# A hybrid decoder layer on one core: gates by one Silu activation, rotations read out of SBUF, and a planner that issues each instruction when its inputs are there

## The chip, the core and the metric

The kernel runs on one core of one Trainium2 chip. The number that counts is the device time of one execution in microseconds (us), from three runs of the kernel before: 2657.21, 2661.30 and 2662.37, so the median is 2661.3 us. A core has a matrix engine (PE, with its weight loads shown as PEld), a vector engine (DVE), a scalar engine for activations (ACT), a general engine (POOL) and a queue engine that only starts DMAs (SP). Each of them works off its own list of instructions in the order in which they stand in it. If the first one in the list has to wait, all behind it wait too.

## What is computed

The reference is one step of a layer with 1024 prompt tokens and 8 decode tokens, 1032 columns in all, with 2048 features. Cut to what matters:

```python
u = rmsnorm(h, g_ln); z = u @ w_in                      # 2048 x 8320
# group A (16 heads of 64): token shift, decay, delta-rule state, per-head norm
xs = feats + mu_shift * (prev - feats)                  # feats = first 3200 columns of z
y_a, wkv_T = rwkv7_scan(wkv0, r, w, k, v, -kk, kk * a)
y_a = (head_norm(y_a) + bonus) * silu(z[..., OFF_GA:OFF_GA + D_A])
# group B (4 heads of 256): rotated q and k, chunked retention, per-head norm
qb = rotary_every_two(q, pos); kb = rotary_every_two(k, pos) / 16
y_b = head_norm(retention(ret0, qb, kb, vb)) * silu(gb)
h = h + concat(y_a, y_b) @ w_out
h = h + sigmoid(h @ w_ple_gate) * (p @ w_ple)
y = rmsnorm(h, g_final)                                 # and the new states
```

## The kernel before, in words

Activations lie transposed, 128 features on the partitions and the 1032 tokens along the free axis, cut into three groups of 344. A projection block makes 128 output features: for each group, 16 steps of three matmuls (`whi` with the high half of u, `whi` with its low half, `wlo` with the high half), 48 matmuls of 344 columns into one PSUM bank. There are 65 such blocks of `w_in`, then 16 of `w_out` (blocks o0 to o15) and 16 of `w_gate` (g0 to g15). Two blocks of p @ w_ple stand in between, one ahead of o0 and one ahead of g0; they have short groups of six matmuls and use four banks.

The eight PSUM banks are two for projections (`pj`), three for everything short (`g`), two for the chain of group A and the states of group B (`ch`), and one for outputs (`y`). Since `pj` has two banks, a group can start only when the bank of the group before the last has been read out; the reading is called the eviction. What an eviction does depends on the block:

- r, k and v of group A (`shifted`, L840): ACT copies the bank to an SBUF tile `z`, POOL forms a difference, DVE makes the shift.
- the gates (`gate_evict`, L867, eight blocks, and `gb_evict`, L346, eight blocks): ACT writes sigmoid(x) into `sgt` (or `g` for the last block), then DVE multiplies it by x, which it reads from the same bank once more.
- q and k of group B (`rope_evict`, L1308): two halves of a head are two blocks; DVE reads the bank twice and multiplies it with the cosine and sine table `tb`, which a DMA on SP fetches per group; POOL adds the products of the second half to `Q` or `K`.
- o0 to o15 (`h_evict`, L1909): DVE adds the residual, ACT and DVE split the sum into two fp16 halves.

While PE runs projections, background generators feed it short work between two steps: `front_gen` (L970) makes a head pair's inputs, `chain_gen` (L1150) walks the sequential state through 16 chunks, `norm` (L1224) is its head norm, `ret_gen` (L1507) and `post_gen` (L1579) are retention and its norm, `dec_gen` and `dec_a_gen` do the decode tokens. The weights are prepared three steps ahead: `ahead` (L395) loads a block and takes its sum of squares (`wjunk`), a tiny matmul adds it over the partitions (`g<-wsr`), `split_w` (L490) makes `whi` on ACT and `wlo` on DVE.

The order of the instructions is made by a planner in the kernel itself (`Driver`, L64). It walks through the program with its own table of costs and a clock `dv.t`, which follows PE. A background generator yields what it waits for: `when(t, more)` (L656) means "go on when the planner believes tile t is written, and `more` us after that"; `yield "g"` means "when a `g` bank is free". What it issues then is put at the end of the engines' lists. `later(t, fn)` (L521) puts off the second half of an eviction to 1.4 us after `t`, or to the next eviction if that comes first (`flush`, L517). So the numbers in `when` set no time on the chip. They set the place of an instruction in its list.

Around the step from o0 to o1: `chase` (L554) runs o0 through the 16 parts of its input as they get ready, on both `pj` banks and the `y` bank; `first_out` (L1936) then waits until the last part is made (`out_open`, L1888) and evicts. The parts are called `mix`; the last two are made by `gated` (L1619): DVE multiplies by the gate, ACT writes the high half, DVE the low half, six times. o1 waits for the `pj` banks, and for its own weights, whose preparation starts only after that of o0.

All instructions of DVE, ACT and POOL carry the line of one recording helper, L256; matmuls carry L303 and transposes L308; DMAs L226. So the rows below are told apart by tiles.

## Time and profile before

| | us |
|---|---|
| median of three runs | 2661.3 |
| the profiled execution, its own time | 2656.86 |
| its span, first to last instruction | 2655.1 |
| PE busy | 2560.7 |
| DVE busy | 1622.2 |
| ACT busy | 1200.8 |
| POOL busy | 541.4 |

The span of the profiled execution is 1.8 us less than its time. PE is busy for 96% of the span, so the table is read from what PE does not do: the 94 us in which it is idle, and the stretches in which its clock is granted at half. A row of the waits names who ended an idle time of an engine; a row of the timeline has the idle time ahead of an instruction in brackets.

### The profile page before, as it was taken

The page shows a single profiled execution, that of the slowest core. Times are in us where ns is not written, and L with a number is a line of the kernel's source. Part 1 is how long each engine was busy: PE and PEld are TensorE (multiplying, and loading weights), DVE is VectorE, ACT ScalarE, POOL GpSimd, SP SyncE. Part 2 cuts the span into 40 slices and gives each one's busy share as a digit, 9 for nine tenths or more (in the row PEclk, how much of TensorE's full clock was granted, in tenths as well). Part 3 has the DMA queues.
Part 4 walks back from the last instruction along what each step waited for, and adds up shares of the span by engine and source line. Part 5 has one row for each costly group of instructions (what it writes and reads, how often), then busy time and mean ns, then how long its engine had stood idle before and what let it go on. Part 6 is the DMA issues. An engine that isn't in the chain of part 4 may idle for free. (4 is left out here: it accounts for less than half of the span.)

```text
span 2655.1 us, 47348 instructions
## 1 busy us (share of the span) xinstructions
PE 2560.7 (96%) x19480; PEld 1761.7 (66%) x19480; DVE 1622.2 (61%) x3458; ACT 1200.8 (45%) x1901; POOL 541.4 (20%) x558
## 2 busy tenths in 40 slices
PE   7899999999999999999999999999989999999996
PEld 4566666666676666666677676776756666666664
DVE  7559685868777766767446957454554443454434
ACT  7564545454645445462343344534443333353433
POOL 3322231322313132220111301111000000033323
PEclk9999999999999999999999999999999999999998
DMA  7222121221212222223334347443443322432314
GB/s 277 78 66 78 59 75 57 78 73 63 77 64 77 80 77 79 64 67 97 98 113 156 101 158 249 141 139 135 156 151 114 110 98 72 154 126 96 110 66 144
DMA packets 146745, 283.67 MB, mean 107 GB/s; under 512 B 62568, under 2 KB 100520, under 8 KB 131424
## 3 DMA queue, kind: packets, MB, share of 16 engines
q1 hardware_dynamic: 132160, 178.91, 20.6%
q10 hardware_dynamic: 14368, 101.73, 11.3%
q8 instruction: 153, 2.51, 0.4%
q14 instruction: 64, 0.52, 0.1%
HBM read 212.78 MB, written 67.55 MB: 106 GB/s over the span
## 5 line engine op out<-in xcount | busy, mean ns | idle before, releaser
L303 PE MATMUL pj<-u,whi 128*128 128x344 f16 x6176 | 1369.1, 310 | 27.0 <-POOL u L256 10.0
L303 PEld LDWEIGHTS <-whi 128*128 128x128 f16 x9408 | 895.8, 99 | 480.7 <-issue 60.0
L303 PE MATMUL pj<-u,wlo 128*128 128x344 f16 x3088 | 951.0, 310 | 0.3 <-DVE wlo L256 0.2
L303 PEld LDWEIGHTS <-wlo 128*128 128x128 f16 x4704 | 460.9, 98 | 232.0 <-DVE wlo L256 4.7
L303 PE MATMUL pj<-mix,whi 128*128 128x344 f16 x1504 | 331.9, 311 | 6.4 <-ACT whi L256 6.4
L303 PE MATMUL pj<-hh,whi 128*128 128x344 f16 (+3 forms) x1536 | 335.0, 309 | 0.2 <-ACT whi L256 0.2
L256 DVE SCALAR_TENSOR_TENSOR wlo<-raw,so,whi 128x512 f16<-128x512 f32 (+1 forms) x398 | 308.2, 806 | 25.6 <-ACT whi L256 24.8
L256 ACT ACTIVATE wjunk<-raw 128x1024 f16<-128x1024 f32 (+1 forms) x188 | 196.1, 1043 | 158.2 <-DVE raw L256 144.6
L256 ACT ACTIVATE whi<-raw,so 128x1024 f16<-128x1024 f32 (+2 forms) x200 | 218.5, 1121 | 87.9 <-DVE so L256 80.3
L303 PE MATMUL pj<-hh,wlo 128*128 128x344 f16 (+3 forms) x768 | 237.3, 309 | 0.4 <-DVE wlo L256 0.4
L303 PE MATMUL pj<-mix,wlo 128*128 128x344 f16 x752 | 231.0, 311 | 2.4 <-DVE wlo L256 2.4
L256 ACT ACT_TABLE_LOAD x150 | 192.4, 1283 | 3.6 <-PEq L2174 0.7
L256 POOL TENSOR_TENSOR H<-H,sgt 128x344 f32<-128x344 f32 (+3 forms) x45 | 55.1, 1226 | 559.2 <-DVE sgt L256 480.4
L256 DVE TENSOR_TENSOR tm<-LT,Z 128x8 f32<-128x8 f32 (+15 forms) x128 | 135.3, 1057 | 1.1
L256 DVE TENSOR_TENSOR sgt<-sgt,xr 128x344 f32<-128x344 f32 (+3 forms) x48 | 26.2, 545 | 155.9 <-ACT sgt L256 142.1
L256 POOL TENSOR_TENSOR d<-z 128x344 f32<-128x344 f32 (+1 forms) x75 | 70.5, 940 | 245.9 <-ACT z L256 191.7
L256 DVE SCALAR_TENSOR_TENSOR hr<-pj,winv,xr 128x344 f32<-128x344 f32 x47 | 27.0, 575 | 133.2 <-PE pj L303 133.2
L256 ACT ACTIVATE AV<-ch 64x128 f32<-64x128 f32 x120 | 32.2, 268 | 164.4 <-PE ch L303 164.2
L256 DVE SCALAR_TENSOR_TENSOR Sbd<-Sbd,DC,ch 64x64 f32<-64x64 f32 x240 | 66.8, 278 | 60.9 <-PE ch L303 57.6
L256 ACT ACTIVATE z<-pj,winv 128x344 f32<-128x344 f32 x74 | 40.1, 546 | 125.5 <-PE pj L303 105.8
L256 ACT ACTIVATE sgt<-pj,winv 128x344 f32<-128x344 f32 (+4 forms) x93 | 50.5, 542 | 89.2 <-PE pj L303 71.6
L256 POOL TENSOR_TENSOR rl<-y,rh 128x344 fp32r<-128x344 f32 x24 | 27.1, 1128 | 305.3 <-DVE rh L256 252.3
(319 smaller groups left out, 3383.7 us busy)
## 6 DMA issues: line engine op xcount, KB each, us to landing
raw<-in_w_in ACTq DMA_DIRECT2D x63, 1024.0 KB, 5.1
raw<-in_w_out ACTq DMA_DIRECT2D x16, 1024.0 KB, 5.0
raw<-in_w_gate ACTq DMA_DIRECT2D x16, 1024.0 KB, 4.7
x<-in_xT SPq DMA_DIRECT2D x16, 516.0 KB, 10.2
tb<-in_rq SPq DMA_DIRECT2D x24, 344.0 KB, 4.4
tb<-in_rk SPq DMA_DIRECT2D x24, 344.0 KB, 3.6
xr<-in_xT SPq DMA_DIRECT2D x16, 516.0 KB, 4.6
d_h<-hr SPq DMA_DIRECT2D x16, 516.0 KB, 2.9
```

The source lines that it names most:

```text
L256: return f(*a, **k)
L303: PE.matmul(out, lhsT, rhs, **kw)
```

## The change

Silu takes the place of sigmoid and a multiplication: ACT writes x * sigmoid(x) from the bank, and DVE does not touch the bank. A rotation's bank is copied by ACT to a tile `z`, and DVE multiplies out of SBUF. `later` takes a margin, 0.2 us where 1.4 stood. In `front_gen`, `rest_gen`, `norm`, `post_gen` and others a `when` stands ahead of each instruction on another engine, and the margins of most matmuls that wait for a split in two halves go from 1.2 or 1.4 us to 0.2; those for `kq`, `Vt` and `yr` go up to 1.2, 1.2 and 3.5. In `post_gen` the low half is made by DVE, where POOL made it. In the chain the copy `AV` is issued one step later (`put`). A rotation's third table is loaded after the first group's rotation. o1 gets banks of its own (`second_out`: both `ch` banks and a `g` bank), is computed before o0 is evicted, and its weights are loaded and squared ahead, as are those of g1.

```diff
@@ preps
                 if raw is None:
                     raw = load_raw(src)
+                    if late is not None:
+                        dv.spawn(ahead(specs, n + 1))
                     yield
@@ later
-    def later(t, fn):
+    def later(t, fn, more=0.2):
...
-            yield when(t, 1.4)
+            yield when(t, more)
@@ gate_evict
-            S_.activation(sg[:, 0:n], ps[:, 0:n], AF.Sigmoid, scale=inv)
+            S_.activation(sg[:, 0:n], ps[:, 0:n], AF.Silu, scale=inv)
+            if gi == 2:
+                S_.activation(gdec[:, p, :], ps[:, n:gw], AF.Identity, scale=inv)
             def fin():
-                if gi == 2:
-                    V.tensor_scalar(out=gdec[:, p, :], in0=ps[:, n:gw], scalar1=inv, scalar2=None, op0=ALU.mult)
-                V.scalar_tensor_tensor(out=sg[:, 0:n], in0=ps[:, 0:n], scalar=inv, in1=sg[:, 0:n],
-                                       op0=ALU.mult, op1=ALU.mult)
                 SP.dma_start(out=d_gate[p][:, g0:g0 + n], in_=sg[:, 0:n])
@@ norm (of group A)
-        halves(y2, Yh, Yl)
-        yield when(Yl, 1.4)
+        yield when(y2, 0.0)
+        V.tensor_copy(out=Yh, in_=y2)
+        yield when(Yh, 0.0)
+        G.tensor_tensor(out=Yl, in0=y2, in1=Yh, op=ALU.subtract)
+        yield when(Yl, 0.2)
         yield "g"
         yv = gtile()
@@ rope_evict
-            for i in {0: (0, 1), 1: (2,), 2: ()}[gi]:
-                st[i] = fpool("tb").tile([P, 2, GW], F32, name="tb", bufs=2)
...
+            if gi == 0:
+                table_of(0)
+                table_of(1)
...
+            z = zg.tile([P, GW], F32, name="z")
+            S_.activation(z, ps, AF.Identity, scale=inv)
+
+            def fin():
+                rotate()
+                if gi == 0:
+                    table_of(2)
...
-                V.scalar_tensor_tensor(out=dst[:, 0, gs], in0=ps, scalar=inv, in1=tb[:, 0, :], op0=ALU.mult, op1=ALU.mult)
+                    V.tensor_tensor(out=dst[:, 0, gs], in0=z, in1=tb[:, 0, :], op=ALU.mult)
...
+            later(z, fin)
@@ gb_evict
-            S_.activation(g, ps, AF.Sigmoid, scale=inv)
+            S_.activation(g, ps, AF.Silu, scale=inv)
             def fin():
-                V.scalar_tensor_tensor(out=g, in0=ps, scalar=inv, in1=g, op0=ALU.mult, op1=ALU.mult)
@@ cap_gen, ret_gen, dec_a_gen
-        yield when(kq, 0.1)
+        yield when(kq, 1.2)
-                    yield when(Vt, 0.1)
+                    yield when(Vt, 1.2)
-        yield when(yr, 0.4)
+        yield when(yr, 3.5)
@@ post_gen, twice
-            halves(y2[:, 0, 0:gw], hi, lo)
-            yield when(lo, 1.2)
+            halves(y2[:, 0, 0:gw], hi, lo, V)
+            yield when(lo, 0.2)
@@ first_out, second_out
-        while not out_open():
+        def results():
+            while not out_open():
+                yield 0.2
+            evict_all(h_evict(0), *got)
+            done.add("out0")
+        dv.spawn(results())
+        dv.spawn(no_hurry(MAIN["n"] + 4))
+
+    def second_out():
+        hi, lo, inv = W.pop(("o", 1))
+        ps = [chp.tile([P, 512], F32, name="ch"), chp.tile([P, 512], F32, name="ch"), gtile()]
+        for gi, (g0, gw) in enumerate(GROUPS):
+            yield from mm3(ps[gi][:, 0:gw], hi, lo, MX[0], MX[1], KT, g0, gw)
+        while "out0" not in done:
             dv.t += 0.3
             yield
-        evict_all(h_evict(0), *got)
-        dv.spawn(no_hurry(MAIN["n"] + 4))
+        evict_all(h_evict(1), ps, inv)
```

Three places show how the lists change. The first is the list of SP at the end of group A, where the last head pair is inverted (`d_X`, `XN`, `d_Z`, `X`) while the first head's q is rotated. `tb<-in_rq` are its tables. Before:

```order
L226 DMA d_mxa<-Y 128x512
L226 DMA d_X<-tm 64x512
L226 DMA XN<-d_X 32x64x16
L226 DMA d_Z<-Z 128x512
L226 DMA tb<-in_rq 128x2x344 x3
L226 DMA X<-d_Z 32x8x32 x4
```

And of the change, at the same place:

```order
L226 DMA d_gb<-sgt 128x344 x2
L226 DMA tb<-in_rq 128x2x344 x5
L226 DMA d_X<-tm 64x512
L226 DMA XN<-d_X 32x64x16
L226 DMA d_Z<-Z 128x512
L226 DMA tb<-in_rq 128x2x344
L226 DMA X<-d_Z 32x8x32 x8
```

Five of the six tables of this head now stand ahead of the round trip through `d_X`. Before, three stood behind it.

The second place is PE's list at the end of o0 (`mix_20584` and `mix_20608` are its last input part) and the start of o1. Before:

```order
L303 MATMUL y<-mix_20584,wlo 128x344
L303 LDWEIGHTS exact
L303 MATMUL g<-wsr,exact 128x2
L303 LDWEIGHTS whi
L303 MATMUL pj<-mix_20261,whi 128x344
```

Of the change:

```order
L303 MATMUL y<-mix_20608,wlo 128x344
L303 LDWEIGHTS whi
L303 MATMUL ch<-mix_20285,whi 128x344
L303 LDWEIGHTS whi
L303 MATMUL ch<-mix_20285,whi 128x344
L303 LDWEIGHTS wlo
L303 MATMUL ch<-mix_20285,wlo 128x344
L303 LDWEIGHTS exact
L303 MATMUL g<-wsr,exact 128x2
```

o1 goes to `ch`, and the sum of its weights is no longer the last thing ahead of it; the `g<-wsr` here is that of o2.

The third place is ACT's list over the same time: `mix<-Y` are the high halves of the last input parts, `wjunk` and `whi` belong to weights, `y<-Y`, `rs` and `tl` to the last norm. Before:

```order
L256 ACTIVATE rs<-rs 128x344
L256 ACT_TABLE_LOAD
L256 ACTIVATE tl<-eps_rms 128x1
L256 ACTIVATE mix_20566<-Y,sret 128x344
L226 DMA raw<-in_w_out 128x2048
L256 ACTIVATE mix_20566<-Y,sret 128x344 x2
L256 ACTIVATE mix_20584<-Y,sret 128x344 x3
L256 ACTIVATE wjunk,wss_20934<-raw 128x1024 x2
```

Of the change:

```order
L256 ACTIVATE tl<-eps_rms 128x1
L226 DMA raw<-in_w_out 128x2048
L256 ACTIVATE whi<-raw,so_20837 128x1024 x2
L256 ACTIVATE mix_20591<-Y,sret 128x344 x3
L256 ACTIVATE mix_20608<-Y,sret 128x344
L256 ACTIVATE wjunk,wss_20960<-raw 128x1024 x2
L256 ACTIVATE wsr<-wss_20960 128x2
L256 ACTIVATE mix_20608<-Y,sret 128x344
```

The high half of o1's weights stands ahead of all six `mix` activations now, and the squares of o2's weights stand between the fourth and the fifth.

## Rows read from the trace of the kernel before

**Rows 1.** The page: busy time of each engine, share of the span and instructions.

```profile
PE 2560.7 (96%) x19480; PEld 1761.7 (66%) x19480; DVE 1622.2 (61%) x3458; ACT 1200.8 (45%) x1901; POOL 541.4 (20%) x558
```

**Rows 2.** Busy time by stretch: group A, the end of group A, group B, the step to `w_out`, `w_out`. Columns: the stretch, its length, busy us (instructions) of PE, PEld, DVE, ACT and POOL, the granted share of PE's full clock, DMA share, GB/s.

```profile
95.00:1250.00 1155.00, 1140.36 (x9571) 784.84 (x9569) 845.43 (x1819) 577.35 (x926) 280.98 (x329) 1.00 0.23 72
1250.00:1350.00 100.00, 96.19 (x869) 66.68 (x868) 45.65 (x132) 29.79 (x54) 14.47 (x15) 0.97 0.33 99
1350.00:1905.00 555.00, 544.87 (x3817) 394.57 (x3816) 328.19 (x779) 238.05 (x386) 82.80 (x76) 0.99 0.45 151
1905.00:1967.00 62.00, 47.68 (x301) 30.19 (x300) 36.60 (x82) 34.61 (x57) 4.58 (x3) 0.92 0.58 199
1967.00:2250.00 283.00, 283.00 (x1953) 189.92 (x1951) 122.27 (x253) 95.74 (x137) 0.00 (x0) 1.00 0.30 100
```

**Rows 3.** The waits of PE between 95 and 1905 us: PE and its line, who ended the wait, us in total, times, the longest.

```profile
PE pj L303 <- DVE sgt L256: 5.8, 5, 1.9
PE pj L303 <- DVE z L256: 5.2, 2, 3.7
PE pj L303 <- ACT z L256: 2.4, 1, 2.4
PE g L308 <- DMA yr<-d_yd: 2.4, 1, 2.4
PE g L308 <- ACT V L256: 2.1, 2, 1.1
PE g L303 <- POOL rl L256: 1.6, 2, 1.0
...
PE g L303 <- DVE kq L256: 1.4, 2, 0.9
```

**Rows 4.** Timeline at the first rotation's second half (start, length, engine, line, operation, tiles, count, and in brackets the idle time ahead of it and who ended it), and below it the busy time and clock of the stretch behind it, columns as in Rows 2.

```profile
1257.07 5.69 SPq L226 DMA_DIRECT2D tb<-in_rq  x3
...
1261.14 1.06 DVE L256 SCALAR_TENSOR_TENSOR z<-pj,winv,tb 128x344 f32<-128x344 f32 x2 [10.76 <-DMA tb<-in_rq]
...
1262.25 0.47 PE L303 MATMUL pj<-u,whi 128*128 128x344 f16 x2 [3.74 <-DVE z L256]
...
1262.60:1269.40 6.80, 6.80 (x51) 4.22 (x50) 3.80 (x8) 4.45 (x6) 2.71 (x4) 0.50 0.50 123
```

**Rows 5.** Timeline of PE at the decode tokens' `yr`, and the stretch behind it, columns as in Rows 4.

```profile
1546.05 0.99 PE L308 MATMUL g<-con,yr 8*128 8x8 f32 x8 [2.35 <-DMA yr<-d_yd]
...
1545.90:1552.70 6.80, 6.65 (x30) 4.53 (x31) 1.01 (x5) 2.26 (x4) 0.00 (x0) 0.50 1.02 416
```

**Rows 6.** Timeline at the step from o0 to o1: PE, then ACT, then DVE, and the busy time and clock of the stretch.

```profile
1950.57 0.17 PE L303 MATMUL g<-wsr,exact 128*128 128x2 bf16 x1
1957.14 0.75 PE L303 MATMUL pj<-mix,whi 128*128 128x344 f16 x2 [6.40 <-ACT whi L256]
1960.29 0.47 PE L303 MATMUL pj<-mix,wlo 128*128 128x344 f16 x1 [2.40 <-DVE wlo L256]
...
1955.95 2.17 ACT L256 ACTIVATE whi<-raw,so 128x1024 f16<-128x1024 f32 x2
...
1957.29 2.28 DVE L256 TENSOR_TENSOR raw<-raw,rf_mix 128x2048 f32<-128x2048 f32 x1
...
1955.50:1965.70 10.20, 6.16 (x21) 2.98 (x22) 6.21 (x7) 5.22 (x8) 0.00 (x0) 0.50 0.38 125
```

**Rows 7.** Groups of instructions over the whole span: line, engine, operation, output <- inputs, partitions x elements, count | busy us, mean ns of one | idle time before them.

```profile
L256 ACT ACT_TABLE_LOAD x150 | 192.4, 1283 | 3.6 <-PEq L2174 0.7 <-DVE winv L256 0.2
...
L256 ACT ACTIVATE z<-pj,winv 128x344 f32<-128x344 f32 x74 | 40.1, 546 | 125.5 <-PE pj L303 105.8 <-PE g L303 6.5 <-DVE winv L256 5.1
...
L256 POOL TENSOR_TENSOR Yl<-y,Yh 128x512 fp32r<-128x512 f32 x16 | 34.1, 2134 | 217.8 <-DVE Yh L256 217.8
...
L256 POOL TENSOR_TENSOR rl<-y,rh 128x344 fp32r<-128x344 f32 x24 | 27.1, 1128 | 305.3 <-DVE rh L256 252.3 <-DVE h L256 25.1 <-ACT whi L256 18.2
...
L256 DVE SCALAR_TENSOR_TENSOR z<-pj,winv,tb 128x344 f32<-128x344 f32 x48 | 25.3, 567 | 23.8 <-DMA tb<-in_rq 10.8 <-issue 5.5 <-PE pj L303 4.0
...
L256 DVE TENSOR_TENSOR sgt<-sgt,xr 128x344 f32<-128x344 f32 x42 | 21.7, 518 | 133.5 <-ACT sgt L256 119.7 <-issue 13.8
...
L256 DVE SCALAR_TENSOR_TENSOR sgt<-pj,winv,sgt 128x344 f32<-128x344 f32 x37 | 21.0, 568 | 1.4 <-ACT sgt L256 0.9
```

**Rows 8.** Timeline of POOL's subtraction `rl` and of the DVE instruction beside it, at two places.

```profile
1661.25 1.05 DVE L256 SCALAR_TENSOR_TENSOR z<-pj,winv,tb 128x344 f32<-128x344 f32 x2
...
1661.47 0.92 POOL L256 TENSOR_TENSOR rl<-y,rh 128x344 fp32r<-128x344 f32 x1 [3.27 <-DVE rh L256]
...
1906.83 2.15 DVE L256 TENSOR_TENSOR raw<-raw,rf_mix 128x1920 f32<-128x1920 f32 x1
...
1907.09 2.67 POOL L256 TENSOR_TENSOR rl<-y,rh 128x344 fp32r<-128x344 f32 x1 [9.32 <-DVE rh L256]
```

**Rows 9.** Timeline of PE in the short groups ahead of o0 and at the last of o0's 16 steps (nine matmuls), and of DVE at the last `mix`.

```profile
1915.69 0.45 PE L303 MATMUL pj<-pt,whi 128*128 128x344 f16 x2 [2.80 <-DVE g L256]
...
1920.19 0.45 PE L303 MATMUL pj<-pt,whi 128*128 128x344 f16 x2 [0.84 <-DVE sgt L256]
...
1949.26 0.46 PE L303 MATMUL pj<-mix,whi 128*128 128x344 f16 x2
...
1945.89 0.57 DVE L256 SCALAR_TENSOR_TENSOR mix<-Y,sret,mix 128x344 f16<-128x344 f32 x1
```

More of the change, by code (lines that the diff above doesn't have):

```diff
@@ L981, in front_gen @@
             S_.activation(sq, k[:, ts], AF.Square, scale=vcol("k_k", p))
-            halves(sq, rh, rl)
+            yield when(sq, 0.0)
+            V.tensor_copy(out=rh, in_=sq)
             sg, a, Gt = scr(0), scr(1), scr(2)
+            yield "g"
             pw = gtile()
             lora_mm(pw, p, 0, ts)
+            yield when(rh, 0.0)
+            G.tensor_tensor(out=rl, in0=sq, in1=rh, op=ALU.subtract)
+            yield when(pw, 0.0)
             S_.activation(sg, pw, AF.Sigmoid, scale=lsi[:, 0:1], bias=vcol("w0", p))
+            yield when(sg, 0.0)
             V.tensor_tensor_scan(out=Gt, data0=rmask, data1=sg, initial=0.0, op0=ALU.mult, op1=ALU.add, est=1.14)
@@ L1102, in bkn_gen @@
                 tr(ps[:, ci * P:ci * P + P], bk[:, ci, :])
+            yield when(ps, 0.1)
             S_.activation(bn, c4(ps), AF.Copy)
@@ L1117, in rest_gen @@
             rs.append((scr(2 * hf, F32R), scr(2 * hf + 1, F32R)))
-            halves(r[:, hf * HB:hf * HB + HB], *rs[hf])
+            V.tensor_copy(out=rs[hf][0], in_=r[:, hf * HB:hf * HB + HB])
+            yield when(rs[hf][0], 0.0)
+            G.tensor_tensor(out=rs[hf][1], in0=r[:, hf * HB:hf * HB + HB], in1=rs[hf][0], op=ALU.subtract)
             yield
@@ L1161, in a2v, with put @@
                    start=True, stop=True, skip_group_check=True)
+            return ps, None
+        def put(c, ps):
             av = None
@@ L1189, in chain_gen @@
             yield
+            if c < 15:
+                nxt = put(c + 1, nxt[0])
             mm(ps[:, 2 * P:3 * P], bn[:, ci, :], uv[:, ci, :], start=True, stop=True)
@@ L1232, in norm @@
         Y = og.tile([P, HB], F32, name="Y")
+        yield when(yc, 0.0)
         S_.activation(y2, yc, AF.Square)
@@ L1314, in pre @@
                 B[which, h] = (fpool("F3") if q else fp).tile([P, 2, T], F32, name=which, tag="F1" if which == "K" else "F3" if q else "F0")
[L1315 to L1318 removed]
+            if gi == 0:
+                table_of(0)
+                table_of(1)
@@ L1593, in norm @@
             mm_exact(pm[:, 0:gw], ones_r, hi, lo)
+            yield when(pm, 0.0)
             for vh in range(2):
@@ L1605, in norm @@
             mm_exact(pq[:, 0:gw], ones_r, hi, lo)
+            yield when(pq, 0.0)
             rs = one.tile([P, GW], F32, name="rs")
@@ L1609, in norm @@
             if h == 3 and g0:
-                table(AF.Sigmoid)
+                table(AF.Silu)
+            yield when(rs, 0.0)
             V.tensor_tensor(out=Y[:, :, gsl], in0=Y[:, :, gsl], in1=rs[:, 0:gw].unsqueeze(1).to_broadcast([P, 2, gw]), op=ALU.mult)
@@ L1947, in items_out @@
         for m in range(KT):
-            spec.append((("o", m), A["w_out"][m], rf_mix, None, None if m else mix_known, None if m else (lambda: ("gate", 7) in done, None)))
-            run = (lambda m=m: proj_gen(("o", m), MX, h_evict(m))) if m else first_out
+            spec.append((("o", m), A["w_out"][m], rf_mix, None, {0: mix_known, 1: lambda: ("gate", 7) in done}.get(m), None if m else (lambda: ("gate", 7) in done, None)))
+            run = {0: first_out, 1: second_out}.get(m, lambda m=m: proj_gen(("o", m), MX, h_evict(m)))
             it.append((("o", m), run, None, None))
```

73 lines of the change are left out of this document (43 added, 30 removed).

## The prediction, made before the changed kernel ran

> **What bounds the kernel.** I read the page's busy times first: PE is at work for 2560.7 of 2655.1 us [rows 1], so no other engine bounds the whole, and the change takes no matmul away. Only three things can give time back: PE's idle time (94 us), stretches at half clock, and new waits with the other sign. I then asked for busy time by stretch [rows 2]. In `w_out` PE is busy for all 283.00 us with 1953 matmuls, 0.145 us each; nothing is to be had there, and a group of 48 lasts 7.0 us. Idle are 14.6 us in group A, 3.8 at its end, 10.1 in group B and 14.3 in the 62 us around the step to `w_out`. The other 51 us (94.4 less these 42.9) lie at the kernel's two ends and around g0, and the change hardly touches those.
>
> The waits of PE [rows 3] say what the idle time in the middle is: banks of `pj` that DVE or ACT had not read out (5.8, 5.2 and 2.4 us), and short matmuls put too early in PE's list (`yr` 2.4, `V` 2.1, `rl` 1.6, `kq` 1.4). The clock adds to it: after the wait of 3.74 us [rows 4] and that of 2.35 us [rows 5] it is granted at half (1.2 of 2.4 GHz) for 6.80 us each, with PE busy throughout. That costs 3.4 us a time.
>
> **The change, part by part.** All terms are us of PE's time.
>
> *Gates.* 48 DVE multiplications out of PSUM (0.568 each [rows 7]) go, 27 us of DVE, and with them the second reading of the bank. The waits under `sgt` are 5.8 in five times [rows 3]. ACT stays in the way, with 0.55 instead of 0.55 + 0.57 before the bank is free. I take 5.0. For the wait of 2.80 ahead of o0, which DVE's `g` ends [rows 9], only that 0.57 comes off, since both banks wait for ACT first: 0.5. Silu needs a table of its own: the built program has 162 table loads on ACT where 150 stood, 12 at 1.283 [rows 7], 15.4 us of ACT. ACT is at 45% [rows 1], and a bank may stay unread for nearly 7.0 us, so I cost them at nothing. If that cover is missing at every one of them it is 15.4. Bounds: 0 to 6.4, less 15.4.
>
> *Rotations.* ACT gains 48 copies at 0.546 [rows 7], 26.2 us; DVE's 96 instructions stay, 0.567 out of PSUM, 0.518 by the nearest row with both inputs in SBUF [rows 7]. What counts is that the bank no longer waits for the table. At 1257 SP stood behind the round trip through `d_X` and issued three tables late, DVE waited 10.76 for them, and PE 3.74 for DVE [rows 4]. In the new list five tables stand ahead of that trip, and ACT frees the bank without any. The two waits under `z` are 5.2 [rows 3]; with the half clock behind the first 8.6. I take 8.5. Bounds 0 (ACT is as late as DVE was) to 8.6.
>
> *Margins made wider.* `yr` moves by 3.1 against a wait of 2.35: 2.35 and its half clock, 5.75 [rows 5]. `kq` moves by 1.1 against 1.4 in two waits, `Vt` by 1.1 against 2.1 in two [rows 3]. Whole: 9.2; I take 9.0. What stands behind these matmuls in PE's list is projection work, which simply comes first now. Bounds 6 to 9.2.
>
> *Margins made narrower.* In `norm` (16 halves) and `post_gen` (24 sums) the matmul behind a split moves 1.0 to 1.2 closer to it. Everything behind it on PE waits with it if it is early. The 16 subtractions `Yl` on POOL take 2.134 in the mean [rows 7], yet before no wait of PE is put down to them [rows 3]. The 24 `rl` go from POOL (1.128) to DVE, 0.518 by the nearest row [rows 7], so half of that lost margin comes back at once. The bounds are 0 and 16 x 1.2 + 24 x 1.0 = 43. I take 5, since no `Yl` and only two `rl` of 24 were late before. The 1.6 of `rl` I leave as it is. The many new `when`s ahead of ACT, DVE and POOL instructions keep an engine from standing before an input that isn't there; of the 2.4 under ACT `z` I take 1.0 for that.
>
> *The step from o0 to o1.* o0's last matmul is done by 1950.74, and the first 21 of o1 fill the time to 1965.7, when the clock is back at full [rows 6]. They are worth 21 x 0.145 = 3.0, so 11.9 is lost: 6.40 and 2.40 of waits, the rest at half clock. The new list starts o1 on `ch`, its weights ready. What was behind the wait moves ahead of it, though: the product `raw` (2.28), the squares `wjunk` and two `whi` (2.17) [rows 6], which now stand between the last norm and the six `mix` activations. The last `mix` ended at 1946.46 and PE reads it at 1949.26 [rows 9], 2.8 of slack. Bounds: all the new work falls into gaps (0), or all delays the chain (2.28 + 2.17 of ACT and DVE work ahead of it, and as much again for o2's weights between two `mix`: 8.9, less 2.8: 6.1). I take 3 there. DVE's `raw` also stands before the short groups' evictions, where PE already waited 0.84 for DVE [rows 9]: between 0 and 2.3 more, and with the last norm pushed back by ACT's squares I take 3 for all of it. So 11.9 - 6 = 6, with ends at 3.5 and 11.9. g1's earlier weights: 0 to 1, I take 1.
>
> Sum: 5.5 + 8.5 + 9.0 + 1.0 + 6 + 1 - 5 = 26 us. The profiled execution's own time is 2656.86 (span and 1.8 around it); 26 off is 2630.9. The median of the runs is 4.4 higher, the lowest run 0.4. I add 2 and forecast 2633.
>
> **A rule that speaks against the rotations.** At 1906.83 DVE multiplies two SBUF tiles for 2.15, and POOL's `rl` beside it takes 2.67; at 1661.25 DVE's rotation has one input in PSUM, and the same `rl` takes 0.92 [rows 8]. The Trainium skill has a rule for this (SBUF — State Buffer, "Who interferes with whom"): a DVE instruction with two SBUF inputs shares its second read path with POOL, and one of them is blocked for the whole instruction; with one SBUF input it does not. The trace agrees, 2.67 against 0.92. The change gives all 96 rotations two SBUF inputs, in group B, where POOL adds the products.
>
> **Rivals.**
>
> 1. *POOL held up by the rotations.* Each group's pair of DVE products (2 x 0.518) can hold POOL by 1.04. Somebody waits only at a block's end, where retention reads `Q` or `K`: 8 second halves x 1.04 = 8.3, if all of it lands on PE. The time is then 2633 + 8.3 = 2641. For it: the two `rl` rows. Against it: POOL is busy 82.8 of 555 us there [rows 2], and v's blocks lie between a rotation and retention.
>
> 2. *The banks now wait for ACT.* Gates and rotations end under another name, because ACT stands before something else or loads a table. Then 5.5 + 8.5 are lost: 2647. For it: ACT `z` already has a wait of 2.4 [rows 3], and ACT gets 42 us more to do. Against it: that was one wait in 74 such evictions [rows 3, 7].
>
> 3. *Slower: PE waits at the 40 narrow places.* PE works its list in order, so a planner that believes a split ready too early stops the projections each time. If each place paid 0.9 on average, that is 36 in place of my 5: 2633 + 31 = 2664. It decides the sign from 0.78 a place on (31 gained without that term, over 40). For it: `Yl` takes up to double what quiet POOL work takes [rows 7, 8], and a margin of 0.2 does not cover that. Against it: the planner's distances are long where it must also find a free bank, and the 24 are faster on DVE.
>
> 4. *Better:* nothing new waits at o0 or at the narrow places, 26 + 5 + 6 = 37: 2622.
>
> **How the numbers follow.** The forecast 0.52, its own range 2624 to 2642; rival 1 0.10; rival 2 0.16; rival 3 0.10; rival 4 0.12. A measurement of this kernel can tell about 0.2% from no change, 5.3 us; so faster is below 2656, slower above 2666.6. Faster 0.86, within 0.2% 0.07 (half of rival 3 and a little of rival 2), slower 0.07. The range of 8 in 10 leaves out the far end of rival 3 and the best of rival 4: 2614 to 2654.
>
> **What would show it.** Right: no wait of PE under DVE `sgt` or DVE `z` in group A's end, none for `yr`, full clock around 1260 and 1550, and o1's first matmul within a microsecond of o0's last; ACT with 162 table loads and some 41 us more busy time, DVE some 15 less. The wait at the last `mix`, if my 3 is right, stands under DVE `mix` at the end of o0. Wrong: PE waits under `Yl`, `rl` or ACT `z` in many places (rivals 2, 3), a fall of the clock where there was none, or POOL's `Q` and `K` near 1.5 us each with PE waiting for them.

## The result, and the profile after

The changed kernel takes 2675.6 us (median of 4 runs, 2674.9 to 2676.3); the kernel before, beside it, 2660.0 (4 runs). The ratio is 1.0059, 95% interval 1.0041 to 1.0076: slower by 15.5 us where 27 less was forecast. Of five kernels below (a_nofront, p_before, b_put, b_norm and b_shift) one execution each took over 5000 us, and the medians leave it out. The page, answering [rows 1]:

```profile
PE 2576.1 (96%) x19480; PEld 1760.0 (66%) x19480; DVE 1618.9 (61%) x3426; ACT 1242.4 (46%) x1969; POOL 487.7 (18%) x534
```

PE's busy time is up by 15.4 with the same 19480 matmuls, so the loss isn't read from idle time alone. By stretch, answering [rows 2]:

```profile
95.00:1250.00 1155.00, 1135.70 (x9459) 772.15 (x9457) 814.65 (x1749) 594.13 (x946) 247.60 (x329) 1.00 0.23 72
1250.00:1350.00 100.00, 99.67 (x898) 68.40 (x896) 56.66 (x135) 32.30 (x60) 14.78 (x13) 1.00 0.31 94
1350.00:1905.00 555.00, 539.45 (x3784) 387.78 (x3783) 333.19 (x789) 255.34 (x416) 73.03 (x57) 0.99 0.43 145
1905.00:1967.00 62.00, 54.24 (x343) 36.70 (x341) 41.40 (x91) 32.98 (x56) 0.00 (x0) 0.92 0.63 226
```

Group A has 112 matmuls fewer in the same 1155 us, group B 33 fewer in 555; the end of group A has 0.3 us of idle time left. The waits of PE between 95 and 1905 us, answering [rows 3]:

```profile
PE g L303 <- DVE rh L256: 11.9, 5, 3.9
PE ch L303 <- DVE UV L256: 6.2, 12, 1.9
PE ch L303 <- DVE R L256: 5.3, 11, 0.8
PE g L303 <- DMA X<-d_Z: 2.3, 1, 2.3
PE g L308 <- DVE BK L256: 2.1, 7, 1.0
PE pj L303 <- ACT z L256: 1.7, 2, 1.1
PE g L303 <- DMA XN<-d_X: 1.5, 1, 1.5
PE g L303 <- DVE kq L256: 1.1, 1, 1.1
```

`sgt`, DVE `z` and `yr` are gone. In their place PE waits for the retention norms' split (`rh`), for the chain (`UV`, `R`) and for the inversion of group A (`BK`, `X`, `XN`).

The waits that the forecast priced are gone where they were looked for; whether the parts that it credited took them away is taken up further down. At the end of group A [rows 4] ACT reads the bank in 0.55 as soon as PE has filled it, five tables stand ahead of the round trip, and the clock is full, as it is where `yr` was [rows 5]; ACT's list, SP's list, and two stretches:

```profile
1261.16 0.55 ACT L256 ACTIVATE z<-pj,winv 128x344 f32<-128x344 f32 x1 [6.51 <-PE pj L303]
...
1242.61 20.72 SPq L226 DMA_DIRECT2D tb<-in_rq  x5
...
1262.00:1270.00 8.00, 8.00 (x58) 5.36 (x57) 7.20 (x13) 3.58 (x5) 0.00 (x0) 1.00 0.59 194
1545.00:1553.00 8.00, 8.00 (x61) 5.44 (x59) 3.47 (x12) 5.57 (x8) 0.00 (x0) 1.00 0.90 330
```

At the step to `w_out`, o1's first matmul starts 0.14 after o0's last, where 6.40 and 2.40 were lost [rows 6]:

```profile
1973.85 0.31 PE L303 MATMUL y<-mix,wlo 128*128 128x344 f16 x1
1973.99 0.31 PE L303 MATMUL ch<-mix,whi 128*128 128x344 f16 x1
```

What is new, by the timeline. The longest `rh` wait: PE, then DVE, whose list holds the split behind work that waited 4.55 for a DMA, and the stretch behind it:

```profile
1460.29 0.66 PE L303 MATMUL g<-rh,exact 128*128 128x344 f32 x1 [3.88 <-DVE rh L256]
...
1453.40 1.23 DVE L256 TENSOR_TENSOR dtm<-Sa,rows 128x1024 f32<-128x1024 f32 x1 [4.55 <-DMA Sa<-in_swkv]
...
1459.90 0.34 DVE L256 CAST rh<-y 128x344 fp32r<-128x344 f32 x1
...
1460.20:1463.60 3.40, 3.31 (x10) 1.78 (x11) 3.33 (x7) 0.00 (x0) 0.42 (x1) 0.50 0.01 2
```

The split itself takes 0.34 and 0.52; it is late because DVE's list is: between the end of that wait and the split DVE has no pause of more than 0.4. The short groups ahead of o0 and those ahead of g0: DVE, PE, and at g1 the sum of its weights:

```profile
1935.39 2.50 DVE L256 TENSOR_TENSOR raw<-raw,rf_mix 128x128 f32<-128x128 f32 x2
...
1939.21 0.73 PE L303 MATMUL pj<-pt,whi 128*128 128x344 f16 x2 [3.60 <-DVE sgt L256]
...
2294.47 2.49 DVE L256 TENSOR_TENSOR raw<-raw,rf_h 128x128 f32<-128x128 f32 x2
...
2297.50 0.73 PE L303 MATMUL pj<-pt,whi 128*128 128x344 f16 x2 [2.75 <-DVE sgt L256]
...
2366.95 0.16 PE L303 MATMUL g<-wsr,exact 128*128 128x2 bf16 x1 [2.33 <-ACT wsr L256]
```

In both places the row of 2.50 or 2.49 joins the last 128x128 of this block's weights and all 128x2048 of the next block's, taken early. It stands ahead of the evictions of the short groups, and PE waits for the bank.

The groups that answer to [rows 7]:

```profile
L256 ACT ACT_TABLE_LOAD x162 | 207.8, 1283 | 6.0 <-DVE wlo L256 1.8 <-PEq L2233 0.7 <-DVE winv L256 0.4
...
L256 POOL TENSOR_TENSOR K<-K,z 128x344 f32<-128x344 f32 x24 | 29.5, 1246 | 88.3 <-DVE z L256 88.3
L256 POOL TENSOR_TENSOR Q<-Q,z 128x344 f32<-128x344 f32 x24 | 28.4, 1203 | 183.2 <-DVE z L256 183.2
L256 DVE TENSOR_TENSOR z<-z,tb 128x344 f32<-128x344 f32 x48 | 24.7, 514 | 14.1 <-issue 8.0 <-ACT z L256 3.6 <-POOL mf L256 1.6
L256 POOL TENSOR_TENSOR Yl<-y,Yh 128x512 fp32r<-128x512 f32 x16 | 23.9, 1494 | 124.5 <-DVE Yh L256 90.6 <-DVE h L256 33.9
L256 DVE TENSOR_TENSOR rl<-y,rh 128x344 fp32r<-128x344 f32 x24 | 12.4, 518 | 0.8
```

### The profile page after: what moved, and what is told of

Its sections match the earlier page's. It is cut to its first block, busy times and chain, and to the rows that moved or that the text cites. A ratio compares the mean times of both kernels' runs of the same rounds, so it can differ in the third digit from the quotient of the medians.

```text
span 2673.0 us, 47282 instructions
## 1 busy us (share of the span) xinstructions
PE 2576.1 (96%) x19480; PEld 1760.0 (66%) x19480; DVE 1618.9 (61%) x3426; ACT 1242.4 (46%) x1969; POOL 487.7 (18%) x534
## 4 chain that ended last, share of the span: by engine, by line
PE 82%; DVE 11%; DMA 2%; ACT 2%; issue 2%; POOL 1%; SPq 0%; DVEq 0%; ACTq 0%; POOLq 0%
PE pj L303 66%; PE ch L303 7%; PE g L303 6%; PE y L303 2%; PE g L308 1%; DVE wlo L256 1%; DVE H L256 1%; DVE tm L256 1%; DVE AR L256 1%; DVE F L256 1%; DVE Y L256 0%; DMA mf<-d_mxa 0%; DVE dtm L256 0%; DVE Sbd L256 0%; DVE so L256 0%
## 5 line engine op out<-in xcount | busy, mean ns | idle before, releaser
L256 DVE SCALAR_TENSOR_TENSOR wlo<-raw,so,whi 128x512 f16<-128x512 f32 (+1 forms) x398 | 323.9, 846 | 20.8 <-ACT whi L256 20.3
L303 PE MATMUL pj<-mix,whi 128*128 128x344 f16 x1408 | 309.5, 310 | 0.0
L303 PE MATMUL pj<-mix,wlo 128*128 128x344 f16 x704 | 215.3, 310 | 0.0
L256 ACT ACTIVATE z<-pj,winv 128x344 f32<-128x344 f32 x122 | 66.0, 543 | 225.7 <-PE pj L303 218.9
L256 DVE TENSOR_TENSOR tm<-LT,Z 128x8 f32<-128x8 f32 (+15 forms) x128 | 142.5, 1113 | 1.6
L256 POOL TENSOR_TENSOR d<-z 128x344 f32<-128x344 f32 (+1 forms) x75 | 61.8, 824 | 384.1 <-ACT z L256 266.7
L256 DVE TENSOR_REDUCE Z<-tm 128x4 f32<-128x8 f32 (+15 forms) x128 | 86.5, 676 | 4.4
## 6 DMA issues: line engine op xcount, KB each, us to landing
x<-in_xT SPq DMA_DIRECT2D x16, 516.0 KB, 10.2
```

What stands on the lines that cost most here:

```text
L256: return f(*a, **k)
L303: PE.matmul(out, lhsT, rhs, **kw)
```

## Where the time goes, stretch by stretch

PE's 14,256 projection matmuls come in the same sequence in every kernel here, so the start of a given one is a mark. I took numbers 720, 2448, 6048, 6768, 9504, 9792, 11808 and 14112, which start at 155, 500, 1244, 1404, 1912, 1973, 2268 and 2616 us in the trace before, and subtracted that trace from each of the others. Between 1973 and 2268 (`w_out`) every difference is 0.0, so that column is left out. Background work crosses a mark now and then, and a stretch at half clock more or less is 1.7 to 5.1 us; a figure is good to some 3 us. "Order only" is explained with its runs. Medians are in us.

| kernel | median | 155–500 | 500–1244 | 1244–1404 | 1404–1912 | 1912–1973 | 2268–2616 |
|---|---|---|---|---|---|---|---|
| changed | 2675.6 | +15.3 | +1.3 | −9.7 | +9.6 | −5.5 | +6.9 |
| p_after (order only) | 2654.7 | +8.6 | +1.4 | −10.1 | +1.8 | −6.6 | +3.9 |
| p_after2 (order only) | 2658.2 | +13.5 | +1.3 | −8.2 | −4.7 | −3.9 | +2.5 |
| a_post12 | 2660.8 | +14.2 | +1.4 | −10.1 | −1.6 | −6.9 | +6.0 |
| a_put | 2671.2 | +8.4 | +3.1 | −9.4 | +12.5 | −6.6 | +4.3 |
| a_nofront | 2677.2 | +13.3 | −0.9 | −3.8 | +13.1 | −5.5 | +6.8 |
| a_nonorm | 2653.1 | +11.4 | −4.7 | −9.3 | +1.4 | −6.6 | +6.0 |
| a_noshift | 2663.6 | +15.0 | +3.5 | −8.4 | +3.3 | −6.7 | +6.0 |
| a_later14 | 2660.0 | +17.2 | +1.2 | −6.5 | −6.7 | −6.6 | +5.9 |
| before | 2657 to 2660 | 0 | 0 | 0 | 0 | 0 | 0 |
| p_before (order only) | 2649.1 | +0.3 | −0.5 | −4.7 | −1.9 | −0.2 | +0.7 |
| b_gains | 2641.6 | +1.1 | −8.3 | −0.2 | −5.3 | +2.4 | 0.0 |
| b_put | 2652.9 | +3.2 | −1.3 | −0.3 | −8.6 | −0.3 | +0.5 |
| b_post | 2644.8 | +2.8 | −0.1 | −2.2 | −9.7 | −3.9 | −0.1 |
| b_out | 2656.2 | +4.4 | +0.9 | +2.8 | −1.9 | −6.1 | +6.7 |
| b_norm | 2650.9 | −3.2 | +7.4 | −5.0 | −7.0 | −0.7 | −0.3 |
| b_shift | 2659.2 | +10.9 | +0.8 | −5.7 | −3.4 | −0.3 | +0.1 |
| b_later | 2668.4 | +9.3 | +10.0 | −5.7 | −1.7 | −0.5 | +0.1 |
| c1 | 2633.9 | +0.9 | −7.2 | −1.3 | −9.3 | −5.3 | −0.4 |
| p_c1 (order only) | 2639.1 | +2.7 | −6.4 | −2.6 | −8.9 | −6.6 | +0.6 |

All but the changed kernel were timed in 5 rounds beside the kernel before; intervals stand with the runs, as ratios to it. Beside the changed kernel the one before had 2660.0, beside the others 2657.0 to 2658.4, so a difference between the changed kernel's median and another's is 1.6 to 3.0 us smaller when each is taken against its neighbour. The columns come from one traced execution each. Its time is within 3 us of the kernel's median, but for b_gains (4.2 above it), a_noshift (5.3) and b_out (7.0).

In the changed kernel 40 short matmuls stand ahead of the mark at 500 that stood behind it before, so its first two columns are best read as a sum, 16.6. That sum can be taken apart. A projection matmul's row lasts 0.31 us where the next one starts 0.14 later, so a stop of PE that is shorter than the difference leaves no gap between the rows and counts as busy. From the mark at 155 to that at 1244 PE has 4.8 more of idle time than before and loses 3.4 more at half clock; the other 8.4 lie in rows that count as busy, with the same 9115 matmuls. In the nine kernels with the chain's `put` (the changed one, p_after, p_after2, all with a_ but a_put, and b_put) this last share is 3.4 to 9.0, in the eleven without it −4.5 to 2.7.

## The experiments

Names with a_ are the changed kernel with a part undone, those with b_ the kernel before with a part alone. Three theories: the chain's step (1), the narrower margins (2), and that a planner's new order lands on other waits whatever the part (3).

**a_put, b_put.** The chain's `put` undone, and alone. In the changed kernel `ch<-UV,BN` starts 0.61 us after the last `ch<-R,X` (median of 128 chunks), in the one before 1.18.

```diff
@@ a_put: chain_gen (b_put the other way round)
-            return ps, None
-
-        def put(c, ps):
             av = None
             if c:
...
-            if c < 15:
-                nxt = put(c + 1, nxt[0])
```

> The changed kernel with one part undone: in the chain the copy AV is issued as before, inside the step that starts the next chunk, so that six projection matmuls stand again in PE's list between the two short matmuls ch<-R,X and ch<-UV,BN, where the change leaves three. Theory 1 (the chain's shorter distance stops PE by some 0.1 us in each of 128 chunks, hidden inside matmul rows that count as busy): 2675.6 less 10 to 14, so 2662 to 2666, with PE's busy time back from 2576 to about 2562 and the distance ch<-R,X to ch<-UV,BN back from 0.61 to 1.2 us. Theory 2 (the loss lies in the narrower margins, the retention norms above all): 2673 to 2677, and PE's busy time stays near 2576. Theory 3 (any new order of the planner costs that much): no direction, within 4 us of 2675.6.

> The kernel before with one part of the change alone: the copy AV of the chain issued one step later. Theory 1 (chain): 2660.0 plus 8 to 14, so 2668 to 2674, PE's busy time up by about that and hardly any new idle time; the loss lies between 100 and 1300 us. Theory 2 (margins): within 4 us of 2660.

Measured: a_put 2671.2, ratio 1.0051 (1.0038 to 1.0063), 4.4 less than the changed kernel where theory 1 had 10 to 14, PE busy 2572.8, the distance back at 1.05. b_put 2652.9, 0.9983 (0.9974 to 0.9992): faster, with the distance down to 0.74. Theory 1 falls as the whole cause. The step does have a price, in the rows of group A that count as busy: 8.4 in the changed kernel, 2.7 with `put` undone, 4.4 with `put` alone. In b_put 2.5 less of idle time there and group B's −8.6 outweigh it.

**a_post12, b_post.** The retention norms.

```diff
@@ a_post12: post_gen of the changed kernel, twice
-            yield when(lo, 0.2)
+            yield when(lo, 1.2)
@@ b_post: post_gen of the kernel before, twice, and a when ahead of each next step
-            halves(y2[:, 0, 0:gw], hi, lo)
-            yield when(lo, 1.2)
+            halves(y2[:, 0, 0:gw], hi, lo, V)
+            yield when(lo, 0.2)
```

> The changed kernel with the two margins of post_gen back at 1.2 us (the halves stay on DVE). Theory 1 (chain): within 4 us of 2675.6, since the waits under DVE rh are only 13.7 us in all and some return elsewhere. Theory 2 (narrow margins of the retention norms): 2675.6 less 10 to 17 (11.9 us of waits under rh between 1400 and 1905 us, and the half clock behind two of them, 3.4 each), so 2659 to 2666; the waits under DVE rh shrink to under 4 us.

> The kernel before with the change's part in the retention norms (post_gen) alone: both halves by DVE, the margins 1.2 -> 0.2, a wait ahead of each next step. Theory 2, which the run a_post12 left standing (DVE is behind the planner here, so a margin of 0.2 lets PE stop for it): 2657.7 plus 8 to 15, so 2666 to 2673, with 8 or more us of waits under DVE rh between 1400 and 1905 us where the kernel before has under 2. Rival (the margin hurts only beside the other parts, because ACT and DVE have rotations and gates in another order): within 4 us of 2657.7.

Measured: a_post12 2660.8, 1.0016 (1.0007 to 1.0024), 14.8 less than the changed kernel, as theory 2 said; the table puts 11.2 of it in group B. The `rh` waits did not shrink to under 4, though: one of 6.88 is left, at 1515.77, behind the wide margin. And b_post, the same narrow margin alone, is faster, by 12.3, which neither expectation had: 2644.8, 0.9955 (0.9944 to 0.9967), and between 1405 and 1905 its `rh` waits are 1.6 us. So 0.2 isn't too little in itself. Theory 2 falls in the form "each place has its price".

**b_gains.** Silu, rotations through `z`, the three wider margins, as in the diff ahead of the prediction, on the kernel before.

> The kernel before with the parts of the change for which the prediction counted a gain in the middle of the program, alone: Silu gates, rotations out of SBUF copies, the wider margins of kq, Vt and yr; not the chain's step, not the narrower margins, not o1's banks. The prediction's own terms: 5.5 + 8.5 + 9.0 = 23, so 2637 from a median of 2660.0. A rival (the waits removed come back elsewhere in the list, and only the half clock's two stretches, 6.8 us, stay away): 2650 to 2656. Another (Silu's 12 more table loads and ACT's 41 us more work cost what the rest gains): 2660.

Measured: 2641.6, 0.9940 (0.9927 to 0.9952), 16 of the 23.

**a_nofront, a_nonorm, b_norm.** The new waits and the margin of `front_gen`, and those of `norm`, taken back or put in alone.

```diff
@@ a_nofront: front_gen, rest_gen (a part)
-            yield when(kb, 0.2)
+            yield when(kb, 0.8)
@@ a_nonorm: norm (b_norm the other way round)
-        yield when(Yl, 0.2)
+        yield when(Yl, 1.4)
```

> The changed kernel with its part in front_gen, rest_gen and their transposes undone (no new waits ahead of the ACT, DVE and POOL steps, margin of kb back from 0.2 to 0.8). Between 95 and 520 us the changed kernel is some 15 us behind the one before; if this part is the cause: 2675.6 less 8 to 15, so 2661 to 2667, and the span from 95 to 520 us gets that shorter. If the cause is the chain's step, the norm or the shift, 2671 to 2679.

> The changed kernel with its part in the norm of group A and at the end of the chain undone (margin of Yl back from 0.2 to 1.4, no new waits). The prediction's rival 3 counted 0.9 us for each of these 16 places, so 14 less: 2661. The profile has no wait of PE under Yl, which speaks for no direction: within 4 us of 2675.6.

> The kernel before with the change's part in the norm of group A and at the chain's end alone (margin of Yl 1.4 -> 0.2, a wait ahead of each next step). Undone in the changed kernel it gave back 22.5 us. If it is the price of the 16 places wherever they stand: 2657.1 plus 10 to 20, so 2667 to 2677. Theory 3: no such loss alone, 2647 to 2664.

Measured: a_nofront 2677.2, 1.0078 (1.0065 to 1.0090), no gain. a_nonorm 2653.1, 0.9982 (0.9973 to 0.9991), 22.5 less than the changed kernel. b_norm 2650.9, 0.9979 (0.9970 to 0.9988): alone it doesn't lose either. And 8.2 of what a_nonorm gave back lies in group B, which this part doesn't touch.

**p_before, p_after, p_after2.** One number of the planner's belief, which changes no instruction.

```diff
-                c = (0.001 if psum else 0.00083) * n + 0.1 + (0.05 if psum else 0.09) * ptr + (0.09 if "accum_out" in k else 0.0)
+                c = (0.001 if psum else 0.00083) * n + 0.11 + (0.05 if psum else 0.09) * ptr + (0.09 if "accum_out" in k else 0.0)
```

> The kernel before with nothing changed but one number in the planner's belief: every ACT instruction is taken to be 0.01 us longer, which changes no instruction and shifts the order here and there. Theory 3 (any new order lands on other waits, and single parts can't be read to better than that): the time moves by 5 to 15 us, in either direction. Theory 2 and the theory of the parts (each part has its price wherever it stands): within 3 us of 2657.1.

> The changed kernel with the same number moved (every ACT instruction believed 0.01 us longer). Theory 3: away from 2675.6 by 5 to 20 us, and rather downwards, since 2675.6 would be an unlucky order; towards 2655 to 2668. Theory of the parts: 2672 to 2679.

> The changed kernel with the number moved the other way (every ACT instruction believed 0.01 us shorter). Theory 3: as p_after, 2655 to 2670. Theory of the parts: 2672 to 2679.

Measured: 2649.1, 0.9972 (0.9962 to 0.9983); 2654.7, 0.9991 (0.9982 to 1.0000); 2658.2, 1.0004 (0.9996 to 1.0013). Theory 3 holds: the same instructions in another order differ by 8 us on the kernel before and by 21 and 17 on the changed one (18 and 14 with each taken against the kernel before beside it). Only ACT's table loads follow the order: 162 in the changed kernel and in p_after2, 156 in p_after. In p_after2 the first 1244 us are within 2 us of the changed kernel and group B is 14.3 better; its `rh` waits there:

```profile
PE g L303 <- DVE rh L256: 2.8, 5, 1.0
```

Five waits in both, 11.9 us against 2.8. So of the 15.5 us about as much hangs on the order in which group B happened to come out, and single parts can't be read to better than that from the whole time. The three kernels with 9.6 or more in group B (the changed one, a_put, a_nofront) share a wait that the six others with a_ or p_after lack: DVE waits 4.3 to 5.1 us for `Sa`, in the six 0.9 at most. In the changed kernel a split follows 6.5 us later (1453.40 and 1459.90 above), and PE waits 3.7 to 4.4 for it in the three; with the half clock behind it that is 5.6 of the 14.3. In c1, described below, DVE waits longer for `Sa`, and the next split comes 21.6 us later:

```profile
1447.55 1.23 DVE L256 TENSOR_TENSOR dtm<-Sa,rows 128x1024 f32<-128x1024 f32 x1 [7.32 <-DMA Sa<-in_swkv]
...
1469.11 0.34 DVE L256 CAST rh<-y 128x344 fp32r<-128x344 f32 x1
```

The table can still be read by columns, where a sign repeats in every order.

**b_out.** The banks of o1, and the earlier weights of o1 and g1, alone.

> The kernel before with the banks of o1 and the earlier weights of o1 and g1 alone. The prediction's terms: 6 + 1, so 2657.7 less 7, 2651. By the blocks of the changed kernel, o1 gains 12, but 8.7 goes at the two short blocks ahead of o0 and of g0 where weights' work stands ahead of the evictions, and 7 in the first blocks of w_gate: 2657.7 plus 0 to 4. A rival (those losses come from the order of the other parts): 2646.

Measured: 2656.2, 0.9997 (0.9989 to 1.0006). By its marks 6.1 is gained between 1912 and 1973 and 6.7 lost after 2268. Its waits of PE between 2250 and 2400 us:

```profile
PE pj L303 <- DVE sgt L256: 2.8, 1, 2.8
PE g L303 <- ACT wsr L256: 2.3, 1, 2.3
```

The changed kernel with its eight variants (all with a_ or p_after) and b_out, the ten with g1's weights taken early, lose 2.5 to 6.9 there; the nine others lie within 0.7 of zero. That part is settled.

**a_noshift, b_shift, b_later, a_later14.** What makes 155 to 500 us late.

```diff
@@ a_noshift: shifted, POOL's work at the eviction again; b_shift the other way round, with later's margins
-            later(z, fin, 0.1)
...
+            G.tensor_tensor(out=d[:, 0:n], in0=z[:, 0:n], in1=z[:, 1:1 + n], op=ALU.subtract)
+            later(d, lambda: V.scalar_tensor_tensor(out=dst(g0, n), in0=d[:, 0:n], scalar=vcol("mu", blk), in1=z[:, 1:1 + n],
+                                                    op0=ALU.mult, op1=ALU.add))
@@ b_later: later
-    def later(t, fn):
+    def later(t, fn, more=0.2):
...
-            yield when(t, 1.4)
+            yield when(t, more)
@@ a_later14: later, and the shift's last step
-    def later(t, fn, more=0.2):
+    def later(t, fn, more=1.4):
...
-                                                        op0=ALU.mult, op1=ALU.add), 0.1)
+                                                        op0=ALU.mult, op1=ALU.add))
```

> The changed kernel with its part in the shift of r, k and v undone (POOL's difference d and its copies are issued at the eviction again, as before). Up to 1244 us the changed kernel and its two shifted orders are 10 to 17 us behind the kernel before, the runs of single parts -7 to +5. If the shift is what costs it: at 1244 us within 5 us of the kernel before, and 8 to 15 us less than 2675.6 from that alone. If no part of its own does: still 7 to 17 us behind at 1244 us. The whole time moves with the order of group B, by up to 20 us, and tells less.

> The kernel before with the shift's part and the margin of later (1.4 -> 0.2 or 0.1) alone. If it costs group A by itself: 10 or more us behind the kernel before at 1244 us, and about 2667. If the loss needs several parts together: within 5 us at 1244 us, and 2647 to 2662.

> The kernel before with one number changed: the second half of an eviction is issued 0.2 us after its tile, where 1.4 stood (the default of later). b_shift, which has this and the shift's part, lost 11 us between 155 and 500 us, a_noshift without the shift's part 15. If the margin alone costs it: 8 to 15 us behind the kernel before at 500 us, and 2658 to 2670 in all. If the margin matters only beside new waits elsewhere: within 5 us at 500 us.

> The changed kernel with the margin of later back at 1.4 us, for the shift's last step too. If that margin is what costs group A: under 5 us behind the kernel before at 500 us, where the changed kernel is 15 behind, and about 2660 unless group B finds a better order too (then 2645 to 2655). If it is not: still 10 to 15 behind at 500 us.

Measured: a_noshift 2663.6, 1.0021 (1.0012 to 1.0030), 15.0 behind in that stretch: not the shift by itself. b_shift 2659.2, 1.0001 (0.9992 to 1.0010), 10.9 behind; b_later 2668.4, 1.0039 (1.0025 to 1.0053), 9.3 behind, so the margin of `later` is enough by itself: the eight kernels built on the one before that keep 1.4 lie between −3.2 and 4.4 there. But a_later14, 2660.0, 1.0010 (1.0001 to 1.0019), is still 17.2 behind. It leaves the shift's own first margin at 0.1, as a_noshift leaves `later` at 0.2, so no run takes both out of the changed kernel and nothing else; that rival stands untested. The wait that the changed kernel, its eight variants, b_shift and b_later share is the one for the inverse on its way through DRAM, between 260 and 274 us, in eight of the eleven with half clock soon behind it; here in b_later, from 150 to 500, one of the two at 272.20 and the other at 425.08:

```profile
PE g L303 <- DMA X<-d_Z: 4.4, 2, 2.5
```

The kernel before and c1 have none there. What brings it about in the changed kernel stays open: one number can bring the loss, and taking that number back in most places doesn't remove it.

**c1, p_c1.** b_gains with the retention norms' part, o1's banks and o1's earlier weights; g1's weights and all of group A's new waits, margins and `put` left out.

```diff
@@ c1, beside the parts named
+                    if late is not None and key[0] == "o":
+                        dv.spawn(ahead(specs, n + 1))
```

> The kernel before with the parts that alone did not lose: Silu gates, rotations out of SBUF copies, the wider margins, the retention norms' part, and o1's banks with its earlier weights; without the earlier weights of g1, the chain's step, and everything in group A's front, norm and shift. If the parts' gains mostly add (16 for the first three, 6 at o1, the retention norms' 12 share the waits of group B with the first): 2630 to 2640. If any order is as good as another: 2645 to 2660.

> The kernel c1 with every ACT instruction believed 0.01 us longer, which changes no instruction and shifts the order. If c1's gain is one of its parts: within 8 us of c1. If it is one lucky order: 10 or more above it.

Measured: c1 2633.9, 0.9908 (0.9895 to 0.9922); p_c1 2639.1, 0.9933 (0.9919 to 0.9946). Both beat both kernels: 24.5 and 19.3 us less than the 2658.4 beside them, and they lie 5.2 apart, so c1's gain does not hang on one order. c1's stretches, group A, its end and group B:

```profile
95.00:1250.00 1155.00, 1147.10 (x9609) 788.89 (x9608) 823.31 (x1771) 593.95 (x948) 278.90 (x329) 1.00 0.24 73
1250.00:1350.00 100.00, 99.61 (x903) 69.22 (x901) 48.58 (x131) 40.21 (x72) 19.26 (x16) 0.98 0.32 98
1350.00:1905.00 555.00, 545.32 (x3824) 395.73 (x3823) 337.80 (x813) 260.06 (x430) 66.55 (x54) 0.99 0.45 157
```

38 matmuls more than before in group A's window, 150 more than the changed kernel.

## Why the prediction was wrong, step by step

**Gates (5.5): about right.** No wait under `sgt` is left up to 1905 us; the wait ahead of o0 went from 2.80 to 2.17, 0.6 for the 0.5. The 162 loads cost nothing that shows: ACT's `z` makes PE wait 1.7 where it was 2.4. In b_gains, c1 and p_c1, which have the gates without group A's other parts, group A gains 7.2, 6.3 and 3.7, against 5.0, and no kernel without the gates gains more than 0.2 there. The rows under `sgt` by themselves don't show it: from 5.8 in the kernel before they fell to 3.1 in p_before, 1.5 in b_later, 1.1 in b_shift, 0.2 in b_put and nothing in b_norm, which all keep the old gates, and other waits took their place.

**Rotations (8.5): right for the tie between table and bank, not shown for the time.** The stretch from 1244 to 1404 gains 9.7 in the changed kernel and 3.8 to 10.1 in its eight variants, and no kernel with the new rotations has a wait of the bank under DVE `z` there, though in b_gains and c1 DVE still waits 8.8 and 7.9 for the table. But p_before, b_shift and b_later, with the old rotations, have no such wait either and gain 4.7 to 5.7, and c1 and b_gains gain only 1.3 and 0.2: in b_gains PE waits 1.38 for `X` at 1260.52 and the clock falls all the same, in c1 it is granted at 0.98 with 99.61 busy of 100. So the 3.74 of wait and the 3.4 at half clock hung on the order of the kernel before as well as on this part.

**POOL beside the rotations (rival 1): fell.** `Q` and `K` take 1.203 and 1.246 on POOL, where the groups of the kernel before have 0.969 and 1.048; over all kernels here they take 1.14 to 1.27 with the new rotations and 0.97 to 1.11 with the old. That is about 0.2 each and 0.4 for a pair, under the 1.04 that the rival counted for a pair, and PE waits 0.2 for `K`, once. The Trainium skill (SBUF — State Buffer, "Who interferes with whom") has a DVE instruction with two SBUF inputs contend with one of POOL that reads SBUF. The direction agrees, and what it costs here is 48 x 0.2, some 10 us of an engine that is busy for 18%.

**Rival 2: fell.** Behind the gates and rotations PE waits 1.1 for ACT's `z` once in group B, and the 2.17 for ACT's `g` ahead of o0 that the sum had counted.

**Wider margins (9.0): the waits went, not shown to be these margins' doing.** `yr` and its half clock are gone, `kq` is down to 1.1; c1 gains 9.3 in group B, b_gains 5.3, both with the retention norms' waits counted in. But b_put, b_post and b_norm keep the old margins of `yr`, `kq` and `Vt`, have no wait under `yr` and no half clock in group B either, and gain 8.6, 9.7 and 7.0 there. The rows that this term priced belonged to one order.

**o0 to o1 (6): right in size, in part by luck.** −5.5, and −3.9 to −6.9 in every kernel that has it (b_post has −3.9 without it, no other more than −0.7). The price named for it came too, in the short groups: 3.60 for the bank behind `raw`, where [rows 9] had 0.84. No wait stands at the last `mix`, so the 3 counted there did not come. But the gain of 11.9 counted half clock among its losses, and that did not come back: between the marks at 1912 and 1973 the clock is at half for 10.2 us before and after, now in two stretches that begin at 1938.1 and 1951.7. The two misses cancel.

**g1's weights (1): wrong in sign,** a loss of 6.9. I had followed `raw` ahead of the evictions at o0 and priced it there, and didn't look at g0, where the same edit does the same: 2.75 for the bank, 6.80 at half clock behind it, 2.33 for `wsr`.

**Narrower margins (−5): the step that failed.** It priced each place by what its own row had cost before, and it gave no term to the parts with no row: `put`, `later` at 0.2, the shift, the new `when`s of group A beyond 1.0. The places themselves were nearly harmless (`Yl` is never waited for, and takes 1.494 now, not 2.134; b_post and b_norm alone gain). What the runs show in place of the 5 is the distance from c1, which has the 24 sums of `post_gen` at their narrow margin and leaves out the 16 halves of `norm`, g1's earlier weights and the parts with no row. From c1 to the changed kernel, by the table: 22.9 in group A, 18.9 in group B, −8.4 at group A's end, 7.3 at g0, −0.2 at o1: 40.5 of the 41.7 between their medians. Much of the 18.9 is one order's bad luck, since six of the nine (the changed kernel and its eight variants) have −6.7 to +3.3 in group B and three, those with the wait for `Sa`, 9.6 to 13.1. Group A's part is not luck alone: each of the nine is 6.7 to 18.5 behind the kernel before there. Of its 22.9, 8.9 lie in rows that count as busy, where `put` has its price, 12.3 are idle time and 1.7 half clock; what brings these two about stays open, since no single part taken back brings them down to c1's. As I read it, the parts together pack short work more tightly against the planner's clock, and where DVE is behind that clock, as at 1453, what follows stops PE; no run shows the planner's clock beside the engines'. The mechanism of rival 3, a planner that believes a split ready too early, is the nearest to what happened, under `rh`, at 6 places over the whole span, not at 40; and a price per place does not describe it: the six waits are between 1.2 and 3.9.

**DVE 15 less: wrong for the changed kernel.** It is 3.3 less; in b_gains it is 21.6 less, in c1 18.1. Its 386 `wlo` of 128x512 went from 816 to 857 ns, 15.8 us in all; why, no run tells. ACT's 162 loads and 41.6 more came as forecast.

**The range.** 2614 to 2654 was built from the terms, each with its bounds. A shift of order by itself moved the kernel before by 8 us and the changed one by 21: a term of ±10 of its own was missing. By my estimate it would have put "slower" nearer 0.2 than 0.07, but a range of ±10 more would still not have reached 2675.6. That c1 came out at 2633.9, where the forecast for the changed kernel stood, confirms no single term: at group A's end it gains 1.3, where 7.1 of the rotations' term was counted.

## What to carry to other kernels

Where a planner's beliefs set the order, perturb one belief that changes no instruction before any part is judged: the scatter of those runs is the smallest effect that a single run of a part can show, and marks along the bottleneck engine show which stretch repeats its sign. A row of waits belongs to the order in which it was read: before it is credited to an edit, see whether it stays when the order changes without that edit; much of what stood under `sgt`, `z` and `yr` here did not. A split of 0.34 and 0.52 us was waited for 3.88 because its engine had waited 4.55 for a DMA, so price a smaller margin by how far the producing engine can fall behind, not by the producer's own length. Rows that overlap hide short stops, so compare the distance between marks, and not idle time alone. When an edit is put in at two places, follow it at both.

## What the hardware showed that was not expected

The same wait can be followed by full clock or by half. b_post has the same marks as the kernel before up to 465 us, to 0.1 us; in both PE then waits 2.42 us for ACT's `z` at 488.9. In the trace before the clock stays at full, in that of b_post it is granted at half for 6.80 us. The stretch in the one and in the other:

```profile
488.20:495.00 6.80, 6.13 (x55) 4.58 (x55) 4.35 (x13) 2.56 (x7) 1.90 (x4) 1.00 0.10 35
```

```profile
488.20:495.00 6.80, 6.07 (x30) 4.23 (x30) 3.25 (x9) 2.35 (x6) 1.84 (x4) 0.50 0.12 42
```

30 matmuls in place of 55, some 3 us, which is the +2.8 of b_post in the first column. Part of the scatter between executions of one kernel goes with the clock: of 112 executions of the kernel before, the 13 with a mean granted clock of 0.993 or 0.994 took 2654.2 on average, the 41 with 0.988 to 0.990 took 2658.5. And waits of this length are a gamble: in the changed kernel those of 2.33 and 3.88 us were followed by 3.40 us at half clock, those of 2.75 and 3.60 by 6.80, and one of 2.17 at 1931.86 by none.
